# Block attention of a two-layer mixer: its products as split fp32r matmuls, with the query projection ahead of the block compression

## The chip, the cores and the metric

One core of a Trainium2 chip. The metric is device time in microseconds (us) of one execution. In the rows, PE is the matmul engine (TensorE) and PEld its weight loads, DVE the vector engine, ACT the scalar engine, POOL GpSimd, and SP the queue that issues most DMAs.

## What is computed

256 tokens of width 1024 go through feed-forward layers, a first mixer, and then two equal layers, each with a second mixer between feed-forward parts. The second mixer has three attention branches. The change touches the block attention (`nsa_attention`), which itself sums three parts, weighted by per-token gates; `sel` and `win` are causal attention with keys and values of their own:

```python
q = qk_norm(x @ w_q)            # 8 heads of 64, rope on 16 of them
k_c, v_c = compress(k, v)       # blocks of 16 tokens, stride 8: an MLP with weights w1
o_c = softmax(mask_c(q @ k_c.T / 8)) @ v_c
o_s = softmax(causal(q @ k_s.T / 8)) @ v_s     # 2 groups, 4 heads each
o_w = softmax(causal(q @ k_w.T / 8)) @ v_w
o = g[..., 0] * o_c + g[..., 1] * o_s + g[..., 2] * o_w
```

All of it is fp32. In this cut the two causal parts are written as they come out for 256 tokens.

## The kernel before

The tokens are two tiles `t` of 128. A weight comes by DMA on SP as 128x1024 into `raw` (four buffers), is copied to its high part `hi` in fp32r by ACT (L212) and subtracted to its low part `lo` by DVE (L214). A dense product is three fp32r matmuls of 512 columns (L227 hi by high input, L228 lo by high input, L229 hi by low input). So each weight costs ACT and DVE about a microsecond apiece, and PE works behind both. The order of instructions on each engine is set at build time by a scheduler that follows the program's order and the pools; nothing reorders at run time.

The names in the rows end in the section of the program: `ckv` (keys and values, and the loads and splits of the compression weights w1, L942 to L949, into `gl` tiles), `cmp` (the compression, L951 to L994), `nq` (the query projection, L996 to L1009), `dsa` (another branch), `nsa` (the block attention, L1028 to L1089), `gate` (gate projections, whose matmuls are placed between the small ones of `dsa` and `nsa`), `br` and `wo`. In layer 0 the sections named here lie at about 760 to 905 us, and in layer 1 in the same order at about 1390 to 1535 us.

In `nsa` a score is a plain fp32 matmul of 64 rows and 128 columns (L496), and the product of probabilities and values one of 128 rows and 64 columns (L526). An fp32 matmul leaves two records in the trace. A *unit* here is one score bank of 128x512: four heads of tile 0, or two heads of tile 1. Per unit come a mask matmul (L483), maximum (L502), exponential, four transposes (L462), a copy of these (L470), and the products. Each part's output is then scaled and added on DVE (L1057, L1086, L1087), and the sum is transposed again for the output projection (`tp_gate<-ident,ob_nsa`, L265).

`tc.issue_after(after)` holds the first score matmuls behind the last transpose of the queries. PSUM pools: `at` 2 buffers, `tp` 2, `po` 1, `mm` 3.

Of the kernel before, what the change touches and what calls it, by code (L numbers as in the profile page):

```python
# [8 lines left out]
F32 = mybir.dt.float32  # L9
# [108 lines left out]
class K:  # L118
# [78 lines left out]
    def load(self, w, r0, nk, c0, n, pool=None):  # L197

        nc = self.nc
        raw = self.tile(self.wpool, [P, nk, n], "raw", bufs=RAW)  # L200
        parts, m = ([(w, c0)], n) if not isinstance(w, list) else (w, n // len(w))
        for i, (v, c) in enumerate(parts):
            nc.sync.dma_start(out=raw[:, :, m * i:m * i + m],
                              in_=v[r0:r0 + nk * P, c:c + m].rearrange("(k p) n -> p k n", p=P))
# [516 lines left out]
    def mixer2(self, l, nxt):  # L721
# [7 lines left out]
        with ExitStack() as outer:  # L729
# [44 lines left out]
            wi = [I([P, 8], f"wi{t}") for t in range(2)]  # L774
# [16 lines left out]
            gate = [T([P, 24], f"ngate{t}") for t in range(2)]  # L791
# [18 lines left out]
            for t in range(2):  # L810
# [18 lines left out]
                for r in range(8):  # L829
                    m8 = I([P, 8], "m8", 2)  # L830
                    nc.vector.max(out=m8, in_=acc)
                    nc.vector.match_replace(out=acc, in_to_replace=m8, in_values=acc, imm_value=MARK)
# [70 lines left out]
            kT = T([P, 2, S], "kT")  # L903
            vS = [T([P, 2, P], f"vS{t}") for t in range(2)]

            def k_evac(t, ps, br):
                c0 = 256 * (1 - br)
                k = T([P, 2, 64], "selk", 4)
# [3 lines left out]
                self.transposes([k.rearrange("p g d -> p (g d)")], kT[:, br:br + 1, toks[t]])  # L912

            def c_evac(t, ps):
# [4 lines left out]
                self.scaled(vS[t][:, 0], ps[:, 384:512], xs[t][2])  # L919
# [10 lines left out]
            def s_evac(t, ps):  # L930
                k_evac(t, ps, 1)
                self.scaled(vS[t][:, 1], ps[:, 128:256], xs[t][2])

            self.proj(xs, w, 1792, 256, s_evac)


# [16 lines left out]
            vcW = T([P, 8, 64], "vcW")  # L953
            for v in range(2):
                Xv = XS[:, 2 * v:2 * v + 2].rearrange("p g (c b r) -> p g c b r", b=8, r=2)
                hp = self.at((64, 2, P))
                for a in range(2):
# [7 lines left out]
                    ox = I([P, 8, 2, 32], "PT", 3, F32R)  # L965
# [17 lines left out]
                if v == 0:  # L983
                    kc = I([P, 1, 64], "kc")
                    self.head_norm(kc, cp[:, None, :], 1.0, gC[:, None, :])
                    self.rope(kc, c["cosc"], c["sinc"], 8)
                    kd = I([32, 2, 64], "kd", 2)
                    nc.vector.tensor_copy(kd, kc[:32].to_broadcast([32, 2, 64]))
                    p = self.tp((P, 32))
                    nc.tensor.transpose(p, kd.rearrange("p r d -> p (r d)"), self.ident[:32, :32])  # L990
                    nc.vector.tensor_mul(kcT, p, c["bmk"])
                else:
                    nc.vector.tensor_mul(vcW, cp[:, None, :].to_broadcast([P, 8, 64]),
                                         c["bmv"][:, :, None].to_broadcast([P, 8, 64]))  # L994

            self.sec = "nq"  # L996

            nqT = T([P, 4, S], "nqT")

            def nq_evac(t, ps):  # L1000
                tok = T([P, 4, 2, 64], "tok", 3)
                q = tok.rearrange("p j g d -> p (j g) d")
                self.head_norm(tok, ps.rearrange("p (g j d) -> p j g d", g=2, j=4), xs[t][2],
                               gQ[:, None, None, :].to_broadcast([P, 4, 2, 64]))
                self.rope(q, *cs(t, 16), 8)
                self.transposes([tok[:, j].rearrange("p g d -> p (g d)") for j in range(4)], nqT[:, :, toks[t]])

            self.proj(xs, w, 768, 512, nq_evac)
            after = self.lastT  # L1009

# [3 lines left out]
            for t in range(2):  # L1014
# [4 lines left out]
                rd = T([P, 4], "rdc", 2)  # L1019
                for heads, pt, den in self.softmax_banks(mp, t, [[0, 2], [1, 3]], qk, mask, 0.125, ""):  # L1020
                    nc.vector.reciprocal(rd[:, heads[0]:heads[-1] + 1:2], den)
                    PT = self.prob_T(lp, t, pt, "c", 2)
# [7 lines left out]
            ob = []  # L1030
            for t in range(2):
                gt = gate[t].rearrange("p (h b) -> p h b", b=3)
                sc = self.at((P, P))
                with tc.issue_after(after):
                    nc.tensor.matmul(sc, cb["identb"], cb["cmask"][:, toks[t]], start=True, stop=False)
                for j in range(4):
                    nc.tensor.matmul(sc[:, 32 * j:32 * j + 32], nqT[:, j, toks[t]], kcT, start=False, stop=j == 3)
                s3 = sc.rearrange("p (h k) -> p h k", k=16)
# [7 lines left out]
                rd = T([P, 2, 4], "rdb", 2)  # L1046
                nc.vector.reciprocal(rd.rearrange("p g j -> p j g"), den.rearrange("p (j g) -> p j g", g=2))
                rd8 = rd.rearrange("p g j -> p (g j)")
                nc.vector.scalar_tensor_tensor(out=rd8, in0=rd8, scalar=c["cval"][:, t:t + 1], in1=gt[:, :, 0],
                                               op0=OP.mult, op1=OP.mult)  # L1050
                pcT = T([P, 1, P], "pcT", 2)
                self.transposes([pc.rearrange("p h k -> p (h k)")], pcT)
                po = self.po((P, 8, 64))
                nc.tensor.matmul(po.rearrange("p h d -> p (h d)"), pcT[:, 0], vcW.rearrange("p h d -> p (h d)"),
                                 start=True, stop=True)
                o = L([P, 8, 64], f"ob{t}")
                nc.vector.tensor_mul(o, po, rd8[:, :, None].to_broadcast([P, 8, 64]))  # L1057
                ob.append(o)
            pend = []
            for t in range(2):  # L1060
                gt = gate[t].rearrange("p (h b) -> p h b", b=3)
                nh = 4 if t == 0 else 2
                for br in range(2):
                    group = {}
                    rd = T([P, 8], "rdb2", 3)
                    for j0 in range(0, 4, nh):
                        banks = [[4 * g + j for j in range(j0, j0 + nh)] for g in range(2)]
                        qk = lambda h, t=t, br=br: (nqT[64 * (h // 4):64 * (h // 4) + 64, h % 4, toks[t]],
                                                    kT[64 * (h // 4):64 * (h // 4) + 64, br])
                        for heads, pt, den in self.softmax_banks(mp, t, banks, qk, None, 0.125, "", after=after):  # L1070
                            nc.vector.reciprocal(rd[:, heads[0]:heads[-1] + 1], den)
                            PT = self.prob_T(lp, t, pt, "")
                            self.run(pend)

                            def f(heads=heads, PT=PT, t=t, br=br, group=group):
                                if not group:
                                    group["po"] = self.po((P, 8, 64))
                                for i, h in enumerate(heads):
                                    self.pv(group["po"][:, h], PT, i, t,
                                            lambda b: vS[b][:, br, 64 * (h // 4):64 * (h // 4) + 64])  # L1080
                            pend.append(f)

                    def f(t=t, br=br, group=group, rd=rd, gt=gt):
                        nc.vector.tensor_mul(rd, rd, gt[:, :, 1 + br])
                        tmp = T([P, 8, 64], "rl", 2)
                        nc.vector.tensor_mul(tmp, group["po"], rd[:, :, None].to_broadcast([P, 8, 64]))  # L1086
                        nc.vector.tensor_add(ob[t], ob[t], tmp)  # L1087
                    pend.append(f)
            self.run(pend)  # L1089
# [4 lines left out]
            order = [("c", 2, 2, oc), ("a", 0, 2, oa), ("b", 1, 4, ob)]  # L1094
# [14 lines left out]
            for bi, (name, gi, nk, o) in enumerate(order):  # L1109
                oT = []  # L1110
                for t in range(2):
                    hi = self.tile(late, [P, nk, P], f"oTh{bi}{t}", F32R)
                    lo = self.tile(late, [P, nk, P], f"oTl{bi}{t}", F32R)
                    self.split_T(o[t] if nk == 2 else o[t].rearrange("p h d -> p (h d)"), hi, lo)
# [4 lines left out]
            for bi, (name, gi, nk, o) in enumerate(order):  # L1119
# [3 lines left out]
                ws = [self.load(G("w_br_" + name), k * P, 1, 0, D) for k in range(nk)]  # L1123
# [91 lines left out]
```

## Time and profile before

| | us |
|---|---|
| median of three runs | 1787.68 |
| all three | 1787.64, 1787.68, 1796.57 |
| the profiled execution | 1790.69 |
| its span, first to last instruction | 1788.9 |
| mean granted TensorE clock of the profiled execution | 0.993 of full |

The profiled execution stands 3.0 us above the median, and 1.8 us of it lie outside its span. Times in the rows count from the span's start. Because PE's matmuls are pipelined, a matmul's own duration overlaps the next one's; what it costs is the distance from its start to the next start. The same holds on DVE, by less.

### The profile page before, as it was taken

The page shows a single profiled execution, that of the slowest core. Times are in us where ns is not written, and L with a number is a line of the kernel's source. Part 1 is how long each engine was busy: PE and PEld are TensorE (multiplying, and loading weights), DVE is VectorE, ACT ScalarE, POOL GpSimd, SP SyncE. Part 2 cuts the span into 40 slices and gives each one's busy share as a digit, 9 for nine tenths or more (in the row PEclk, how much of TensorE's full clock was granted, in tenths as well). Part 3 has the DMA queues.
Part 4 walks back from the last instruction along what each step waited for, and adds up shares of the span by engine and source line. Part 5 has one row for each costly group of instructions (what it writes and reads, how often), then busy time and mean ns, then how long its engine had stood idle before and what let it go on. Part 6 is the DMA issues. An engine that isn't in the chain of part 4 may idle for free.

```text
span 1788.9 us, 22896 instructions
## 1 busy us (share of the span) xinstructions
PE 1765.3 (99%) x8595; PEld 1453.9 (81%) x8595; DVE 1079.4 (60%) x1706; ACT 897.2 (50%) x1359; POOL 25.8 (1%) x42
## 2 busy tenths in 40 slices
PE   8999999999999999999999999999999999999999
PEld 7888787788878888787888888888887878888887
DVE  5555566555565555797567555655556975575553
ACT  5444455444444444575555444444544755554442
POOL 0000100000000000000000000000000000000000
PEclk9999999999999999999999999999999999999999
DMA  8665654266556655454255665666555442556653
GB/s 281 183 187 192 190 136 142 90 205 188 181 184 195 183 187 192 143 146 125 72 176 178 210 188 182 204 179 188 182 186 155 142 130 69 179 165 203 186 187 130
DMA packets 154991, 305.07 MB, mean 171 GB/s; under 512 B 14040, under 2 KB 45344, under 8 KB 154880
## 3 DMA queue, kind: packets, MB, share of 16 engines
q1 hardware_dynamic: 154864, 303.61, 55.2%
q8 instruction: 67, 1.10, 0.2%
q14 instruction: 44, 0.36, 0.1%
q10 hardware_dynamic: 16, 0.00, 0.0%
HBM read 302.53 MB, written 1.05 MB: 170 GB/s over the span
## 4 chain that ended last, share of the span: by engine, by line
PE 93%; DVE 3%; DMA 2%; ACT 1%; issue 1%; SPq 0%; POOL 0%; POOLq 0%; ACTq 0%
PE mm_ffn L227 10%; PE mm_ffn L229 10%; PE mm_ffn L228 10%; PE at_ffn L229 9%; PE at_ffn L227 9%; PE at_ffn L228 9%; PE mm_gate L228 3%; PE mm_gate L229 2%; PE mm_gate L227 2%; PE at_nsa L496 1%; PE mm_m L228 1%; PE mm_m L227 1%; PE mm_m L229 1%; PE po_nsa L526 1%; PE tp_ffn L265 1%; PE po_ffn L265 1%
## 5 line engine op out<-in xcount | busy, mean ns | idle before, releaser
L214 DVE TENSOR_TENSOR lo_ffn<-raw_ffn,hi_ffn 128x1024 fp32r<-128x1024 f32 x396 | 482.8, 1224 | 455.1 <-ACT hi_ffn L212 453.8
L212 ACT CAST hi_ffn<-raw_ffn 128x1024 fp32r<-128x1024 f32 x396 | 415.2, 1053 | 506.2 <-PE at_ffn L229 307.6
L227 PE MATMUL mm_ffn<-hi_ffn,xh_ffn 128*128 128x512 f32 x288 | 113.1, 393 | 2.5 <-ACT xh_ffn L306 1.3
L228 PE MATMUL mm_ffn<-lo_ffn,xh_ffn 128*128 128x512 f32 x288 | 112.8, 392 | 0.0
L229 PE MATMUL mm_ffn<-hi_ffn,xl_ffn 128*128 128x512 f32 x288 | 112.7, 391 | 0.0
L228 PE MATMUL mm_ffn<-lo_ffn,ah_ffn 128*128 128x512 f32 x264 | 103.8, 393 | 0.0
L227 PE MATMUL mm_ffn<-hi_ffn,ah_ffn 128*128 128x512 f32 x264 | 103.3, 391 | 0.0
L228 PE MATMUL at_ffn<-lo_ffn,ah_ffn 128*128 128x512 f32 x264 | 103.1, 391 | 0.0
L229 PE MATMUL at_ffn<-hi_ffn,al_ffn 128*128 128x512 f32 x264 | 102.9, 390 | 0.0
L227 PE MATMUL at_ffn<-hi_ffn,ah_ffn 128*128 128x512 f32 x264 | 102.8, 389 | 0.0
L229 PE MATMUL mm_ffn<-hi_ffn,al_ffn 128*128 128x512 f32 x264 | 102.8, 389 | 0.0
L227 PE MATMUL at_ffn<-hi_ffn,xh_ffn 128*128 128x512 f32 x240 | 94.5, 394 | 0.0
L229 PE MATMUL at_ffn<-hi_ffn,xl_ffn 128*128 128x512 f32 x240 | 93.5, 390 | 0.0
L228 PE MATMUL at_ffn<-lo_ffn,xh_ffn 128*128 128x512 f32 x240 | 93.4, 389 | 0.0
L214 DVE TENSOR_TENSOR lo_gate<-raw_gate,hi_gate 128x1024 fp32r<-128x1024 f32 x48 | 58.5, 1218 | 35.5 <-ACT hi_gate L212 35.5
L228 PE MATMUL mm_gate<-lo_gate,xh_ffn 128*128 128x512 f32 x192 | 76.9, 401 | 0.7 <-DVE lo_gate L214 0.7
L227 PE MATMUL mm_gate<-hi_gate,xh_ffn 128*128 128x512 f32 x192 | 76.8, 400 | 0.0
L229 PE MATMUL mm_gate<-hi_gate,xl_ffn 128*128 128x512 f32 x192 | 76.3, 399 | 0.0
L228 PE MATMUL mm_ffn<-lo_ffn,xh_wo 128*128 128x512 f32 x192 | 74.9, 390 | 0.0
L229 PE MATMUL mm_ffn<-hi_ffn,xl_wo 128*128 128x512 f32 x192 | 74.7, 389 | 0.0
L227 PE MATMUL mm_ffn<-hi_ffn,xh_wo 128*128 128x512 f32 x192 | 74.7, 389 | 0.0
L212 ACT CAST hi_gate<-raw_gate 128x1024 fp32r<-128x1024 f32 x48 | 50.4, 1051 | 40.1 <-PE mm_gate L229 38.4
(565 smaller groups left out, 3892.3 us busy)
## 6 DMA issues: line engine op xcount, KB each, us to landing
raw_ffn<-in_ffn_w_gu_dram SPq DMA_DIRECT2D x160, 512.0 KB, 3.7
raw_ffn<-in_ffn_w_down_dram SPq DMA_DIRECT2D x132, 512.0 KB, 3.3
raw_gate<-in_w_gate_dram SPq DMA_DIRECT2D x48, 512.0 KB, 3.6
raw_ffn<-in_ffn_w_gate_dram SPq DMA_DIRECT2D x40, 512.0 KB, 4.2
raw_ffn<-in_ffn_w_up_dram SPq DMA_DIRECT2D x40, 512.0 KB, 3.7
raw_m<-in_w_in_dram SPq DMA_DIRECT2D x22, 512.0 KB, 3.8
raw_ffn<-in_ffn_w_gu_dram SPq DMA_DIRECT2D x32, 256.0 KB, 3.2
raw_wo<-in_w_out_dram SPq DMA_DIRECT2D x16, 512.0 KB, 3.3
```

What stands on the lines that cost most here:

```text
L212: nc.scalar.copy(hi, raw)
L214: nc.vector.tensor_sub(lo, raw, hi.bitcast(F32))
L227: nc.tensor.matmul(out, xh, wh, start=first, stop=False)
L228: nc.tensor.matmul(out, xh, wl, start=False, stop=False)
L229: nc.tensor.matmul(out, xl, wh, start=False, stop=last)
L265: nc.tensor.transpose(p[:, i], src[:, i * P:(i + 1) * P], self.ident)
L496: nc.tensor.matmul(sc[:, i, c], q, k[:, c], start=False, stop=i == len(heads) - 1 and b in (t, None))
L526: self.nc.tensor.matmul(out, PT[:, i * (t + 1) + b], v(b), start=b == 0, stop=b == t)
```

## The change

- The section `nq` moves ahead of the loads and splits of w1 and ahead of `cmp`.
- A transposed query is stored stacked, in `qS`: its high part (ACT copy) in the 64 rows of its group, the low part (DVE subtraction) in the other 64. A key is stored as `kh` (high part in both halves) and `kl` (low part in its own half, zeros from POOL in the other). A score for two key blocks is then two fp32r matmuls of 128 rows and 256 columns.
- Values are split (`vh`, `vl`). The probabilities are multiplied by gate over denominator on DVE before they are transposed, the transposed block is split (ACT copy, DVE subtraction), and six fp32r matmuls of 256 columns per unit add all parts into one `po` bank per tile, already transposed. The scaling and adding of outputs on DVE and the eight transposes of `ob` go.
- The compressed scores become eight matmuls of 16 columns per tile instead of four of 32, their product with the values four of 128 columns instead of one of 512.
- The branch's output weight is loaded as two halves of 64 rows (four more DMAs per layer).

```diff
+            kh = T([P, 2, 2, S], "sT", 1, F32R)
+            kl = T([P, 2, 2, S], "kl", 1, F32R)
...
+                p = self.tp([P, P])
+                nc.tensor.transpose(p, k.rearrange("p g d -> p (g d)"), self.ident)
+                for g in range(2):
+                    own, other = half[g], half[1 - g]
+                    nc.scalar.copy(kh[own, g, br, toks[t]], p[own])
+                    nc.scalar.copy(kh[other, g, br, toks[t]], p[own])
+                    nc.vector.tensor_sub(kl[own, g, br, toks[t]], p[own], kh[own, g, br, toks[t]].bitcast(F32))
...
+            def v_evac(t, ps, br):
+                src = ps.rearrange("p (g d) -> p g d", d=64)
+                hi, lo = vh[t][:, br, 0::2], vl[t][:, br, 0::2]
+                self.scaled(hi, src, xs[t][2])
+                nc.vector.scalar_tensor_tensor(out=lo, in0=src, scalar=xs[t][2], in1=hi.bitcast(F32),
+                                               op0=OP.mult, op1=OP.subtract)
...
+            self.sec = "nq"
+
+            qS = T([P, 8, S], "qS", 1, F32R)
+
+            def nq_evac(t, ps):
...
+                for g in range(2):
+                    own, other = half[g], half[1 - g]
+                    dst = qS[:, 4 * g:4 * g + 4, toks[t]]
+                    nc.scalar.copy(dst[own], p[own])
+                    nc.vector.tensor_sub(dst[other], p[own], dst[own].bitcast(F32))
+
+            self.proj(xs, w, 768, 512, nq_evac)
+            after = self.lastT
...
-            self.sec = "nq"
-
-            nqT = T([P, 4, S], "nqT")
...
-            self.proj(xs, w, 768, 512, nq_evac)
-            after = self.lastT
...
+                for i in range(2):
+                    q = qS[:, 4 * g + j0 + i, toks[t]]
...
+                    with tc.issue_after(after) if t == 1 and i == 0 else nullcontext():
+                        nc.tensor.matmul(sc[:, i], q, hi, start=t == 1 and i == 0, stop=False)
+                    nc.tensor.matmul(sc[:, i], q, lo, start=False, stop=t == 0 and i == 1)
...
+                nc.vector.tensor_mul(pw, pw, rd[:, :, None].to_broadcast([P, n, w]))
...
+                nc.scalar.copy(ph, p)
+                nc.vector.tensor_sub(pl, p, ph.bitcast(F32))
...
+                        nc.tensor.matmul(out, wh, ph[:, x], start=False, stop=False)
+                        nc.tensor.matmul(out, wl, ph[:, x], start=False, stop=False)
+                        nc.tensor.matmul(out, wh, pl[:, x], start=False, stop=last and x == 1)
```

How this moves instructions shows at two places, each told for layer 0. The first is DVE between the low part of the last query weight and the low part of the second gate weight. Before, 27 instructions reach from one start to the other; the last of them, where `gl_ckv` are w1 parts, `zs`, `PT` and `kd` work of the compression, and `lo_gate` is a gate weight's low part:

```order
L948 TENSOR_TENSOR gl_ckv_6744<-raw_ckv_6739,gl_ckv_6744 128x4x128
L1157 TENSOR_SCALAR kd_cmp_6785<-tp_cmp_6782 128x32
L967 TENSOR_TENSOR PT_cmp_6825<-zs_cmp_6821,PT_cmp_6825 128x8x32
L1159 TENSOR_SCALAR kd_cmp_6785<-kd_cmp_6785 128x32
L961 TENSOR_TENSOR zs_cmp_6836<-gl_ckv_6456,peT_pn_5817 128x8x15
L1160 RECIPROCAL kd_cmp_6785<-kd_cmp_6785 128x32
L214 TENSOR_TENSOR lo_gate_7512<-raw_gate_7509,hi_gate_7511 128x1024
```

In the changed kernel 62 instructions lie there; a piece of them, on the way to the second gate low part, `lo_gate_7630` (`cop` is what `PT` was, `qS` the queries' low parts, `gl_nq` a w1 part):

```order
L1019 TENSOR_TENSOR cop_cmp_6937<-zs_cmp_6933,cop_cmp_6937 128x8x32
L462 TENSOR_TENSOR tok_nq_6852<-tok_nq_6852,sm_nq_6859 128x512
L1013 TENSOR_TENSOR zs_cmp_6989<-gl_ckv_6454,peT_pn_5817 128x8x15
L431 TENSOR_TENSOR ropeb_nq_6869<-tok_nq_6852,cf_ffn_1602 128x8x8
L432 TENSOR_TENSOR ropeb_nq_6869<-tok_nq_6852,cf_ffn_1602 128x8x8
L983 TENSOR_TENSOR qS_nq_6746<-tp_nq_6843,qS_nq_6746 64x4x128
L433 TENSOR_TENSOR ropea_nq_6868<-tok_nq_6852,cf_ffn_1602 128x128
L1000 TENSOR_TENSOR gl_nq_6904<-raw_nq_6899,gl_nq_6904 128x4x128
L434 TENSOR_TENSOR tok_nq_6852<-ropea_nq_6868,ropeb_nq_6869 128x8x16
```

All eight w1 low parts (three before), all of the queries' normalisation, rope and split (none before) and eight `zs` additions now stand between the two weights.

The second place is PE, at the first use of that gate weight. Before:

```order
L227 MATMUL mm_gate_7489<-hi_gate_7493,xh_ffn_5696 128x512
L228 MATMUL mm_gate_7489<-lo_gate_7494,xh_ffn_5696 128x512
L229 MATMUL mm_gate_7489<-hi_gate_7493,xl_ffn_5697 128x512
L227 MATMUL mm_gate_7489<-hi_gate_7511,xh_ffn_5696 128x512
L228 MATMUL mm_gate_7489<-lo_gate_7512,xh_ffn_5696 128x512
L229 MATMUL mm_gate_7489<-hi_gate_7511,xl_ffn_5697 128x512
```

In the changed kernel:

```order
L233 MATMUL mm_gate_7607<-hi_gate_7629,xh_ffn_5696 128x512
L233 MATMUL mm_gate_7608<-hi_gate_7629,xh_ffn_5771 128x512
L1021 MATMUL at_cmp_6917<-gl_nq_6885,cop_cmp_6922 64x256 x2
L978 MATMUL tp_nq_6843<-ident,tok_nq_6821 128x128 x4
L1021 MATMUL at_cmp_6917<-gl_nq_6885,cop_cmp_6922 64x256 x2
L1021 MATMUL at_cmp_6917<-gl_nq_6888,cop_cmp_6922 64x256 x4
L1021 MATMUL at_cmp_6917<-gl_nq_6893,cop_cmp_6937 64x256 x4
L1021 MATMUL at_cmp_6917<-gl_nq_6896,cop_cmp_6937 64x256 x4
L978 MATMUL tp_nq_6874<-ident,tok_nq_6852 128x128 x4
L1028 MATMUL tp_cmp_6950<-cf_ffn_1602,kd_cmp_6948 128x32 x2
L234 MATMUL mm_gate_7607<-lo_gate_7630,xh_ffn_5696 128x512
```

From the first use of the last query weight's low part to this matmul PE had 37 matmuls and now has 52: seven more gate matmuls of 512 columns and the eight query transposes; the 16 `at_cmp` are in both.

## Rows read from the trace of the kernel before

**Rows 1.** The page's first part: busy time, share of the span and instructions of each engine.

```profile
PE 1765.3 (99%) x8595; PEld 1453.9 (81%) x8595; DVE 1079.4 (60%) x1706; ACT 897.2 (50%) x1359; POOL 25.8 (1%) x42
```

**Rows 2.** Groups by line on PE: out<-in, shape, count | busy us, mean ns.

```profile
L496 PE MATMUL at_nsa<-kT_ckv,nqT_nq 64*128 64x128 f32 x192 | 28.5, 292 | 0.0
L526 PE MATMUL po_nsa<-vS_ckv,PT_nsa 128*128 128x64 f32 x192 | 27.0, 271 | 0.0
...
L1037 PE MATMUL at_nsa<-kcT_cmp,nqT_nq 128*128 128x32 f32 x32 | 4.1, 272 | 0.0
...
L265 PE MATMUL tp_gate<-ident,ob_nsa 128*128 128x128 f32 x16 | 2.2, 279 | 0.0
```

**Rows 3.** PE's timeline in `nsa`: start us, us, instruction.

```profile
840.00 0.38 PE L483 MATMUL at_nsa<-cb 128*128 128x512 bf16 x1
840.31 1.16 PE L496 MATMUL at_nsa<-kT_ckv,nqT_nq 64*128 64x128 f32 x8
841.39 1.13 PE L1054 MATMUL po_nsa<-vcW_cmp,pcT_nsa 128*128 128x512 f32 x2
...
864.83 1.00 PE L526 MATMUL po_nsa<-vS_ckv,PT_nsa 128*128 128x64 f32 x8
865.67 0.27 PE L483 MATMUL at_nsa<-cb 128*128 128x256 bf16 x1
```

**Rows 4.** PE's timeline in `ckv`, first and last of a run of 41.

```profile
782.50 0.28 PE L227 MATMUL mm_ckv<-hi_ckv,xh_ffn 128*128 128x256 f32 x1
...
787.28 0.28 PE L228 MATMUL mm_ckv<-lo_ckv,xh_ffn 128*128 128x256 f32 x1
```

**Rows 5.** Windows: us, busy us of PE, PEld, DVE, ACT, POOL, PEclk, DMA share, GB/s.

```profile
760.00:770.00 10.00, 10.00 (x65) 8.98 (x64) 9.86 (x29) 5.97 (x12) 0.00 (x0) 1.00 0.53 155
...
800.00:810.00 10.00, 9.66 (x57) 7.73 (x56) 9.84 (x29) 7.71 (x16) 0.62 (x2) 1.00 0.69 218
...
850.00:860.00 10.00, 10.00 (x73) 7.93 (x72) 6.59 (x17) 5.95 (x26) 0.00 (x0) 1.00 0.17 53
```

**Rows 6.** DVE's timeline in `ckv`, `cmp` and `nq`: start us, us, instruction.

```profile
793.86 0.16 DVE L425 TENSOR_TENSOR ropeb_ckv<-selk_ckv,cf_ffn 128x16 f32<-128x16 f32 x1
...
794.37 0.34 DVE L453 SCALAR_TENSOR_TENSOR selk_ckv<-mm_ckv,rs_ffn,gS_pn 128x128 f32<-128x128 f32 x1
...
797.49 1.23 DVE L214 TENSOR_TENSOR lo_nq<-raw_nq,hi_nq 128x1024 fp32r<-128x1024 f32 x1
...
801.36 1.22 DVE L214 TENSOR_TENSOR lo_gate<-raw_gate,hi_gate 128x1024 fp32r<-128x1024 f32 x1
802.50 0.42 DVE L967 TENSOR_TENSOR PT_cmp<-zs_cmp,PT_cmp 128x256 fp32r<-128x256 f32 x1
802.83 1.29 DVE L948 TENSOR_TENSOR gl_ckv<-raw_ckv,gl_ckv 128x512 fp32r<-128x512 f32 x2
804.03 0.90 DVE L961 TENSOR_TENSOR zs_cmp<-gl_ckv,peT_pn 128x120 f32<-128x120 f32 x3
804.87 0.67 DVE L948 TENSOR_TENSOR gl_ckv<-raw_ckv,gl_ckv 128x512 fp32r<-128x512 f32 x1
...
806.82 1.16 DVE L214 TENSOR_TENSOR lo_gate<-raw_gate,hi_gate 128x1024 fp32r<-128x1024 f32 x1
...
811.14 0.48 DVE L453 SCALAR_TENSOR_TENSOR tok_nq<-mm_nq,rs_ffn,gQ_pn 128x256 f32<-128x256 f32 x1
811.53 0.15 DVE L442 TENSOR_TENSOR sm_cmp<-sm_cmp,sm_cmp 128x1 f32<-128x1 f32 x1
```

**Rows 7.** PE's timeline, the first use of the second gate low part, in both layers.

```profile
808.03 0.50 PE L228 MATMUL mm_gate<-lo_gate,xh_ffn 128*128 128x512 f32 x1 [0.34 <-DVE lo_gate L214]
...
1435.95 0.50 PE L228 MATMUL mm_gate<-lo_gate,xh_ffn 128*128 128x512 f32 x1 [0.32 <-DVE lo_gate L214]
```

**Rows 8.** Windows and PE's timeline in the first mixer, after a wait.

```profile
214.15 0.50 PE L228 MATMUL mm_m<-lo_m,xh_ffn 128*128 128x512 f32 x1 [2.69 <-DVE lo_m L214]
...
215.40:218.80 3.40, 3.40 (x9) 2.65 (x8) 2.82 (x6) 2.25 (x4) 0.00 (x0) 0.50 0.88 242
```

More of the change, by code (lines that the diff above doesn't have):

```diff
@@ L201, in load @@
         parts, m = ([(w, c0)], n) if not isinstance(w, list) else (w, n // len(w))
-        for i, (v, c) in enumerate(parts):
-            nc.sync.dma_start(out=raw[:, :, m * i:m * i + m],
-                              in_=v[r0:r0 + nk * P, c:c + m].rearrange("(k p) n -> p k n", p=P))
+        if isinstance(r0, list):
+            p0 = 0
+            for r, k in r0:
+                nc.sync.dma_start(out=raw[p0:p0 + k, 0], in_=w[r:r + k, c0:c0 + n])
+                p0 += k
+        else:
+            for i, (v, c) in enumerate(parts):
+                nc.sync.dma_start(out=raw[:, :, m * i:m * i + m],
+                                  in_=v[r0:r0 + nk * P, c:c + m].rearrange("(k p) n -> p k n", p=P))
         if pool is None:
@@ L773, in mixer2 @@
             iT = I([P, 3, S], "iT")
-            wi = [I([P, 8], f"wi{t}") for t in range(2)]
+            wi = I([P, 2, 8], "wi")
+            wi = [wi[:, t] for t in range(2)]
             def idx_evac(t, ps):
@@ L790, in mixer2 @@
             dv = [T([P, 64], f"dv{t}") for t in range(2)]
-            gate = [T([P, 24], f"ngate{t}") for t in range(2)]
+            gate = T([P, 2, 24], "ngate")
+            gate = [gate[:, t] for t in range(2)]
             def dsa_evac(t, ps):
@@ L990, in mixer2 @@
                     nc.tensor.transpose(p, kd.rearrange("p r d -> p (r d)"), self.ident[:32, :32])
[L991 removed]
+                    nc.vector.tensor_copy(kcT, p)
                 else:
[L993 to L1009 removed]
+                    for g in range(2):
+                        nc.vector.tensor_mul(vcW[:, :, g], cp[:, None, :].to_broadcast([P, 4, 64]),
+                                             c["bmv"][:, 4 * g:4 * g + 4, None].to_broadcast([P, 4, 64]))
             self.sec = "dsa"
@@ L1018, in mixer2 @@
                 mask = M[t][:, None, :].to_broadcast([P, 2, P * (t + 1)])
-                rd = T([P, 4], "rdc", 2)
+                rd = self.sm(4, "rdc")
                 for heads, pt, den in self.softmax_banks(mp, t, [[0, 2], [1, 3]], qk, mask, 0.125, ""):
                     nc.vector.reciprocal(rd[:, heads[0]:heads[-1] + 1:2], den)
-                    PT = self.prob_T(lp, t, pt, "c", 2)
+                    PT = self.tile(lp, [P, 2 * (t + 1), P], "rl", bufs=2)
+                    self.transposes([pt[:, i, b * P:(b + 1) * P] for i in range(2) for b in range(t + 1)], PT)
                     for i, h in enumerate(heads):
@@ L1028, in mixer2, with compressed @@
             self.sec = "nsa"
[L1030 to L1033, printed above, removed]
+            obT = [[L([P, 4, P], f"ob{n}{t}", 1, F32R) for n in "hl"] for t in range(2)]
+            pend = []
+            def compressed(t, po, gt):
+                sc = self.at((P, 4, 2, 16))
                 with tc.issue_after(after):
-                    nc.tensor.matmul(sc, cb["identb"], cb["cmask"][:, toks[t]], start=True, stop=False)
+                    nc.tensor.matmul(sc.rearrange("p j g k -> p (j g k)"), cb["identb"], cb["cmask"][:, toks[t]],
+                                     start=True, stop=False)
                 for j in range(4):
-                    nc.tensor.matmul(sc[:, 32 * j:32 * j + 32], nqT[:, j, toks[t]], kcT, start=False, stop=j == 3)
-                s3 = sc.rearrange("p (h k) -> p h k", k=16)
+                    for g in range(2):
+                        nc.tensor.matmul(sc[:, j, g], qS[:, 4 * g + j, toks[t]].bitcast(F32),
+                                         kcT[:, 16 * g:16 * g + 16], start=False, stop=j == 3 and g == 1)
+                s3 = sc.rearrange("p j g k -> p (j g) k")
                 mx = self.sm(8, "mx")
@@ L1045, in mixer2 @@
                 nc.vector.tensor_reduce(out=den, in_=pc, axis=AX.X, op=OP.add)
[L1046 to L1049, printed above, removed]
+                rd = self.recip(den, 8, "rdb")
+                r3 = rd.rearrange("p (j g) -> p j g", g=2)
@@ L1054, in mixer2 @@
[L1054 to L1059, printed above, removed]
+                for j in range(4):
+                    nc.tensor.matmul(po[:, j], vcW[:, j].rearrange("p g d -> p (g d)"), pcT[:, 0],
+                                     start=j == 0, stop=False)
@@ L1060, in mixer2 @@
             for t in range(2):
                 gt = gate[t].rearrange("p (h b) -> p h b", b=3)
[L1062 to L1088, printed above, removed]
@@ L1089, in mixer2 @@
-            self.run(pend)
+                po = self.po((P, 4, P))
+                compressed(t, po, gt)
+                todo = [(g, j0, br) for g in range(2) for j0 in (0, 2) for br in ([None] if t == 0 else [0, 1])]
+                for k, (g, j0, br) in enumerate(todo):
+                    unit(t, g, j0, br, po, gt, k == len(todo) - 1)
+                self.run(pend)
+                nc.scalar.copy(obT[t][0], po)
+                nc.vector.tensor_sub(obT[t][1], po, obT[t][0].bitcast(F32))
@@ L1122, in mixer2 @@
                 acc = self.accs()
-                ws = [self.load(G("w_br_" + name), k * P, 1, 0, D) for k in range(nk)]
+                if o is None:
+                    ws = [self.load(G("w_br_b"), [(64 * k, 64), (256 + 64 * k, 64)], 1, 0, D) for k in range(nk)]
+                else:
+                    ws = [self.load(G("w_br_" + name), k * P, 1, 0, D) for k in range(nk)]
                 for t in range(2):
```

87 lines of the change are left out of this document (75 added, 12 removed).

## The prediction

> **What bounds the kernel now.** I read the page's busy times first: PE is busy for 1765.3 of 1788.9 us, DVE for 1079.4 and POOL for 25.8 [rows 1]. So a microsecond taken from PE is one gained, as long as its operands are there. Next the groups by line and PE's timeline, to price the products that go and those that come [rows 2 to 4]; the reader is to see starts, not durations, since matmuls overlap. Then windows around the place to which the query projection moves: there DVE is at 9.86 and 9.84 of 10 us, so DVE is the second bound, and PE is barely ahead of it [rows 5]. The starts on DVE price what is put between two weights [rows 6]. What the path is worth there shows in PE's first use of the second gate low part: it already waits 0.34 us in layer 0 and 0.32 in layer 1, for DVE [rows 7]. Since the two layers show the same, each term is worked out for one layer and doubled.
>
> **PE's work, per layer.** Scores: 192 records of two layers, so 96 per layer [rows 2], eight of which take 841.39 - 840.31 = 1.08 us, 0.135 each [rows 3]: 13.0 us go. Probabilities by values: 96 records at (865.67 - 864.83) / 8 = 0.105: 10.1 us go. In their place stand 12 units with four score matmuls and six value matmuls, 120 fp32r matmuls of 256 columns. The nearest rows are the 41 of that size in `ckv`, 40 starts in 787.28 - 782.50 = 4.78 us, 0.1195 each [rows 4]: 14.3 us come. So 8.8 us are saved. The compressed scores go from 16 records [rows 2] to 32, since each query head has a matmul of its own: 16 at 0.105 are 1.7 us back. Their value product keeps its columns and is put at nothing, covered by no one: were it to rise by the 0.03 between the two paces over 16 records, 0.5 us. Eight transposes of `ob` go [rows 2], at 0.105: 0.8. The 12 masks stay; one of 512 columns took 0.31 ahead of a 64-row score [rows 3], against 0.24 by the fp32r pace, so 0.07 each, 0.8. Sum: 8.8 - 1.7 + 0.8 + 0.8 = 8.7 us, **17.4 us less for both layers**.
>
> **The move of the query projection, per layer.** Between the starts of the last query low part (797.49) and the second gate low part (806.82) DVE needs 9.3 us for 27 instructions [rows 6]. Now 62 stand there. Their price from starts [rows 6]: the two weight low parts 1.14 each (802.50 - 801.36), 2.3; sixteen of 512 columns, namely eight w1 parts, two reductions, two multiplications and four query low parts, at 0.60 (two from 802.83 to 804.03), 9.6; four query scalings at 0.39 (811.53 - 811.14), 1.6; eight `zs` at 0.28 (three from 804.03 to 804.87), 2.2; four `cop` at 0.33 (802.83 - 802.50), 1.3. Of the 28 smaller ones, six of 2 to 32 columns take 0.51 (793.86 to 794.37), which would make 2.4; some have 64 or 128 columns, a duration of 0.15 each is nearer to 4.2, and I take 3.6 between these ends. Sum 20.6, which is 11.3 more. PE, for its part, has more to do meanwhile: seven matmuls of 512 columns at 0.23 to 0.24 (two of 256, rows 4) and eight transposes at 0.105, 2.4 us. So PE, which already came 0.34 early, waits 0.34 + 11.3 - 2.4 = 9.2 us; **18.4 for both**. Whether this shows at one gate weight or is spread over two and the high parts on ACT is left open. The work was not new: DVE and ACT did it behind the second gate low part, where PE had split weights in hand. What is late next is the key of the compression, whose chain now stands behind three gate low parts, one more than before: up to 1.1 us at `tp_cmp`, taken at 1.0, 2.0 for both.
>
> **Keys and values.** Four times per layer a key costs two DVE subtractions of 64x128 in place of a copy that ACT and DVE shared, and a value one more instruction of 128x128: ten more per layer, at no more than the 0.34 us that one of 128x128 lasts [rows 6], 3.4 us. They fall where DVE is at 9.86 of 10 [rows 5]. At the lower end they cost nothing, since PE still had 10.00 of 10 there. I take 1.0, 2.0 for both layers, with 0 to 6.8 kept for the range.
>
> **The clock.** In the first mixer a wait of 2.69 us for DVE at 214.15 is followed by a stretch, 215.40 to 218.80, in which the granted clock is 0.50, the 1.2 GHz level, while PE is busy throughout: half of its 3.40 us is lost, 1.7 [rows 8]. The short wait of 0.34 us left the clock at 1.00 in its window [rows 5, 7]. Waits of 9 us in one or two pieces per layer are nearer to the first. Two places per layer make 0 to 6.8 us; I take half, 3.4. The Trainium skill, page "TensorE: Matmul & The Clock Gate", sections "What's actually happening" and "HAM oscillation", says that the half clock is the default, that activity lifts it, and that a wait for data brings it back each time; by it all four would count and the sum be 3.4 us longer. The first mixer agrees with it, the short wait shows its limit.
>
> **What costs nothing.** The scaling of the probabilities and the split of their transposes put 26 DVE instructions of 512 columns per layer where 18 stood, 8 x 0.60 = 4.8 us. The stage is longer than the 25 us between the scores and values of rows 3; over these alone it is 1.9 in 10, on top of the 6.59 of 10 that DVE has there [rows 5]: 8.5 at most, hidden behind gate matmuls. Without this cover all 9.6 would show. The Trainium skill, page "TensorEngine Tiling (Array Packing)", section "PSUM Bottleneck", warns that a faster TensorE can leave PSUM's evacuation as the bound; by it the 17.4 us would not come out, and that is the last rival below. The stage's window speaks against it. POOL's zeros hide in an engine that is 1% busy; the four more DMAs per layer and the query weights, which pass the w1 loads on SP's queue, hide while the DMA share is 0.53 and 0.69 [rows 5]; uncovered, w1 would come late and not a gate weight.
>
> **The sum.** -17.4 + 18.4 + 2.0 + 2.0 + 3.4 = +8.4 us. The profiled execution's 1790.7 becomes 1799.1. It stands 3.0 above the median, so against the median 1787.7 the forecast is **1796.1**. With the unknown terms at their lower ends (no clock, no keys and values, no late chain) it is +1.0, 1788.7; at their upper ends (6.8, 6.8, 2.2) +16.8, 1804.5. About 0.5%, 8.9 us, can be told from no change: 1778.8 and 1796.6 are the bounds, and the forecast lies just inside.
>
> **Rivals.**
> *Slower, through the clock.* PE stops at four places long enough that each is followed by a stretch at 1.2 GHz with PE last. For it speaks the fall after 2.69 us [rows 8]; against it, that a wait split into pieces may leave the clock alone as the 0.34 did. All four falls give 1796.1 + 3.4 = 1799.5, with keys and values at their upper end 1804.3; I put it at 1802, between. It decides once waits and clock together exceed 26.3 us (17.4 + 8.9).
> *Faster: the waits don't form.* The moved work is the same work earlier. If DVE enters the stretch further ahead of PE than before, because PE is held up by its own 15 more matmuls and DVE's queue has no wait for a slow transpose, the 18.4 go and the clock stays: 1787.7 - 17.4 + 4.0 = 1774. Half of the waits give 1783. Against it: DVE at 9.84 of 10 has nothing to run ahead with, and the 0.34 is there already.
> *The products' gain does not appear.* Either a stacked fp32r matmul costs as much as the two records it replaces, or the attention stage waits for its evacuation. Then +8.4 + 17.4: 1813. Rows 4 speak against the first, the window of the stage against the second.
>
> **How the numbers follow.** The forecast's case has 0.60, of which its own range, 1789 to 1804, puts 0.44 within the bounds and 0.16 above. The clock case has 0.20, all slower. Waits that don't form have 0.14: 0.10 faster, 0.04 within. The last has 0.06. So faster 0.10, within 0.48, slower 0.42. The range from 1782 to 1806 leaves out most of the third case below and the fourth above, and a tail of the clock case, together under 0.2.
>
> **What would show it.** In the profile after: scores and value products in groups of 256 columns at 0.12 us from start to start; no multiply-and-add of outputs; PE waits of several us for a gate weight at about 803 to 826 us and again some 628 us later, released by DVE's low part or ACT's high part; DVE at 9.8 or more there; windows with PEclk under 1 right behind. Wrong would be: no PE wait over 1 us there (then 1774), or waits inside `nsa` for probabilities (then the evacuation binds).

## The result, and the profile after

The changed kernel takes **1808.9 us** (median of four runs, 1807.8 to 1810.0) against 1787.7 for the one before; the ratio of the runs is 1.0108, 95% interval 1.0093 to 1.0123. That is slower by 19.3 us on that ratio, above the range of 1782 to 1806. The profiled execution is one at the median, 1808.6.

The first part of its page, which answers to [rows 1]:

```profile
span 1806.7 us, 22854 instructions
...
PE 1758.3 (97%) x8491; PEld 1448.5 (80%) x8491; DVE 1104.0 (61%) x1770; ACT 913.5 (51%) x1405; POOL 29.1 (2%) x54
```

PE is busy for 7.0 us less, in a span that is 17.8 longer: its idle time went from 1788.9 - 1765.3 = 23.6 to 1806.7 - 1758.3 = 48.4, up by 24.8. The groups by line on PE show what replaced [rows 2] (busy us, mean ns):

```profile
L1117 PE MATMUL at_nsa<-sT_ckv,qS_nq 128*128 128x256 f32 x48 | 15.3, 337 | 0.0
L1157 PE MATMUL po_nsa<-cop_nsa,vh_ckv 128*128 128x256 f32 x48 | 15.0, 313 | 0.1
...
L1118 PE MATMUL at_nsa<-kl_ckv,qS_nq 128*128 128x256 f32 x48 | 12.8, 283 | 0.0
...
L1079 PE MATMUL at_nsa<-kcT_cmp,qS_nq 128*128 128x16 f32 x64 | 7.6, 261 | 0.0
```

There are no waits before them to speak of. The list of PE's waits (us in total, times, longest) shows where they went instead:

```profile
PE mm_gate L234 <- DVE lo_gate L220: 11.4, 3, 5.5
PE mm_gate L233 <- ACT hi_gate L218: 7.4, 2, 4.0
...
PE mm_nq L233 <- DVE selk_ckv L434: 2.5, 2, 1.2
...
PE tp_nq L978 <- DVE tok_nq L434: 1.8, 2, 0.9
```

In [rows 7] the second gate low part made PE wait 0.34 and 0.32 us. The same places on PE's timeline after, with a piece of `nsa` that answers to [rows 3]:

```profile
787.29 0.47 PE L233 MATMUL mm_nq<-hi_nq,xh_ffn 128*128 128x512 f32 x1 [1.25 <-DVE selk_ckv L434]
...
806.43 1.22 PE L233 MATMUL mm_gate<-hi_gate,xh_ffn 128*128 128x512 f32 x2 [3.96 <-ACT hi_gate L218]
...
823.14 0.79 PE L234 MATMUL mm_gate<-lo_gate,xh_ffn 128*128 128x512 f32 x1 [5.47 <-DVE lo_gate L220]
...
856.05 0.28 PE L1157 MATMUL po_nsa<-cop_nsa,vh_ckv 128*128 128x256 f32 x1
856.17 0.28 PE L1158 MATMUL po_nsa<-cop_nsa,vl_ckv 128*128 128x256 f32 x1
856.29 0.28 PE L1159 MATMUL po_nsa<-sp_nsa,vh_ckv 128*128 128x256 f32 x1
856.41 0.28 PE L1117 MATMUL at_nsa<-sT_ckv,qS_nq 128*128 128x256 f32 x1
856.52 0.28 PE L1118 MATMUL at_nsa<-kl_ckv,qS_nq 128*128 128x256 f32 x1
...
1443.59 0.76 PE L233 MATMUL mm_gate<-hi_gate,xh_ffn 128*128 128x512 f32 x2 [3.45 <-ACT hi_gate L218]
...
1460.82 0.80 PE L234 MATMUL mm_gate<-lo_gate,xh_ffn 128*128 128x512 f32 x1 [5.47 <-DVE lo_gate L220]
```

Matmuls of 256 columns start 0.12 us apart, as priced. DVE between the two gate low parts of layer 0, on its timeline:

```profile
806.41 1.23 DVE L220 TENSOR_TENSOR lo_gate<-raw_gate,hi_gate 128x1024 fp32r<-128x1024 f32 x1 [1.50 <-ACT hi_gate L218]
...
814.34 0.69 DVE L983 TENSOR_TENSOR qS_nq<-tp_nq,qS_nq 64x512 fp32r<-64x512 f32 x1 [1.60 <-ACT qS_nq L982]
...
821.87 1.22 DVE L220 TENSOR_TENSOR lo_gate<-raw_gate,hi_gate 128x1024 fp32r<-128x1024 f32 x1
```

That is 15.5 us from start to start, 5.5 in [rows 6], and part of it DVE itself waits, for ACT's copy of the transposed queries: the line is long, and it is also held. Windows of the same stretch and of `nsa` (columns as in [rows 5]):

```profile
803.40:806.80 3.40, 0.37 (x1) 0.37 (x2) 1.90 (x6) 1.44 (x3) 0.00 (x0) 0.86 0.48 181
806.80:810.20 3.40, 3.36 (x8) 2.16 (x8) 3.40 (x13) 2.64 (x7) 0.00 (x0) 0.50 0.37 89
810.20:813.60 3.40, 3.40 (x14) 2.73 (x14) 2.53 (x12) 1.05 (x1) 0.62 (x2) 0.63 0.18 70
...
820.40:823.80 3.40, 0.66 (x2) 0.56 (x3) 3.34 (x9) 2.01 (x3) 0.00 (x0) 0.50 0.28 109
823.80:827.20 3.40, 3.40 (x21) 3.36 (x20) 3.37 (x8) 0.76 (x4) 0.00 (x0) 0.62 0.82 228
850.00:860.00 10.00, 10.00 (x69) 8.42 (x67) 8.02 (x20) 7.35 (x29) 0.00 (x0) 1.00 0.39 107
```

The granted clock falls to 0.50, the 1.2 GHz level, twice in each layer here. In the four windows at 0.50 to 0.63 PE's busy time times the missing share is 1.7 + 1.3 + 0.3 + 1.3 = 4.6 us lost, and the same windows of layer 1 give 4.6 again; the last row shows `nsa` at full clock, with DVE at 8.02 of 10 and PE never short of work.

Matching starts of the same matmuls gives the same size for both layers: from 717.89 to 924.67 before and 714.47 to 930.44 after it is +9.2, from there to 1552.61 before and 1568.16 after +9.8, 19.0 in all. So by place, from the first to the last of these points: PE's idle time grows by 23.7 and its busy time falls by 4.8 (826.8 before, 822.0 after). Since the clock added about 2 x 4.6 = 9 to the busy time, PE's work is some 14 us less. The execution of before shown had lost 3.4 us ahead of the first of these points, where the program is the same, most of it in PE's busy time (706.0 against 703.1); that is why the spans differ by less than the medians.

### The profile page after: what moved, and what is told of

It is laid out like the page before. It is cut to its first block, busy times and chain, and to the rows that moved or that the text cites. A ratio compares the mean times of both kernels' runs of the same rounds, so it can differ in the third digit from the quotient of the medians.

```text
span 1806.7 us, 22854 instructions
## 1 busy us (share of the span) xinstructions
PE 1758.3 (97%) x8491; PEld 1448.5 (80%) x8491; DVE 1104.0 (61%) x1770; ACT 913.5 (51%) x1405; POOL 29.1 (2%) x54
## 4 chain that ended last, share of the span: by engine, by line
PE 88%; DVE 6%; DMA 3%; ACT 1%; issue 1%; SPq 0%; POOL 0%; POOLq 0%; ACTq 0%
PE mm_ffn L233 10%; PE mm_ffn L234 10%; PE mm_ffn L235 10%; PE at_ffn L235 9%; PE at_ffn L233 9%; PE at_ffn L234 9%; PE mm_gate L234 3%; PE mm_gate L233 3%; PE mm_gate L235 3%; PE mm_m L234 1%; PE mm_m L233 1%; PE mm_m L235 1%; PE tp_ffn L271 1%; PE po_ffn L271 1%; PE at_m L502 1%
## 5 line engine op out<-in xcount | busy, mean ns | idle before, releaser
L234 PE MATMUL mm_gate<-lo_gate,xh_ffn 128*128 128x512 f32 x192 | 79.6, 414 | 11.5 <-DVE lo_gate L220 11.4
```

Of the source, the lines that this page charges most:

```text
L234: nc.tensor.matmul(out, xh, wl, start=False, stop=False)
```

## The experiments

Each ratio is to the kernel before, of runs on the same chip, with its 95% interval; 0.001 is 1.8 us. Every edit is scheduled anew, so the order of instructions on the engines differs in places from kernel to kernel; where this bears on a reading it is said.

**The two halves of the change.** The first kernel is the changed one with the section `nq` put back behind `cmp`, its text unchanged; the second is the kernel before with only that move.

```diff
-            self.sec = "nq"
-
-            qS = T([P, 8, S], "qS", 1, F32R)
...
-            self.proj(xs, w, 768, 512, nq_evac)
-            after = self.lastT
...
             self.sec = "cmp"
...
+            self.sec = "nq"
+
+            qS = T([P, 8, S], "qS", 1, F32R)
...
+            self.proj(xs, w, 768, 512, nq_evac)
+            after = self.lastT
```

and, in the kernel before:

```diff
+            self.sec = "nq"
+
+            nqT = T([P, 4, S], "nqT")
...
+            self.proj(xs, w, 768, 512, nq_evac)
+            after = self.lastT
...
             self.sec = "cmp"
...
-            self.sec = "nq"
-
-            nqT = T([P, 4, S], "nqT")
...
-            self.proj(xs, w, 768, 512, nq_evac)
-            after = self.lastT
```

> The changed kernel with the query projection put back behind the compression; all else of the change stays. If the move is what costs (through DVE's queue or through the weight buffers), PE's waits for gate weights at 803 to 826 us and 628 us later go, and what is left is the cheaper products: 1771 to 1778 us. If the products or their evacuation cost the time, it stays at 1800 or more with waits inside the block attention.

> The kernel before with only the query projection moved ahead of the w1 loads. If the move is what costs, it alone makes the kernel slower than the changed one, by the products' gain that is missing here: 1812 to 1828 us, with PE waiting several us for gate weights. If the move costs nothing by itself, 1786 to 1790.

e1: 1788.0 us, ratio 0.9987 [0.9974, 1.0001]. e2: 1806.3 us, 1.0094 [1.0069, 1.0118]. The move alone costs 16.8 us, somewhat less than was expected of it; putting it back takes 21.6 off the changed kernel. The waits of PE that e2 has and the kernel before has not:

```profile
PE tp_nq L462 <- DVE tok_nq L428: 5.9, 3, 2.6
PE mm_gate L227 <- ACT hi_gate L212: 4.4, 2, 2.5
```

That is 10.3 us, where the changed kernel waits for 11.4 + 7.4 + 1.8 = 20.6 at the same places. And e1 missed: without the move the products should have made it some 10 to 17 us faster than before, and it is hardly faster at all. Its PE has a wait that the kernel before does not have (the changed kernel has it too, the 1.25 us at 787.29). PE's timeline of e1:

```profile
790.69 0.28 PE L893 MATMUL at_sb<-cop_sb,neg 128*128 128x256 f32 x1
792.58 0.47 PE L233 MATMUL mm_nq<-hi_nq,xh_ffn 128*128 128x512 f32 x1 [1.60 <-DVE selk_ckv L434]
```

What DVE did meanwhile (its timeline):

```profile
790.89 1.02 DVE L895 TENSOR_TENSOR zs_sb<-zs_sb,at_sb 128x256 f32<-128x256 f32 x2 [0.51 <-PE at_sb L891]
...
792.09 0.34 DVE L941 SCALAR_TENSOR_TENSOR vl_ckv<-mm_ckv,rs_ffn,vh_ckv 128x128 fp32r<-128x128 f32 x1
```

And the windows behind it:

```profile
790.00:792.60 2.60, 0.99 (x9) 0.77 (x7) 2.09 (x13) 1.52 (x3) 0.00 (x0) 1.00 0.66 202
790.00:800.00 10.00, 8.39 (x45) 7.15 (x44) 7.02 (x32) 6.15 (x17) 0.56 (x2) 0.83 0.34 105
...
794.50:797.90 3.40, 3.40 (x11) 2.76 (x10) 2.43 (x11) 2.77 (x10) 0.29 (x2) 0.50 0.51 154
```

The wait ends 0.15 us behind L941; the profile names L434, the next in DVE's line, which neither reads `mm` nor feeds the query. The query's first matmul needs a bank of the `mm` pool, which has three; its last reader is the value's low part, read from `mm_ckv` on DVE, and that stands in line behind the additions of another branch and the rope. In the kernel before, a value left that bank by one instruction of ACT. Then the clock falls and 1.7 us more go, in each layer. PE goes on to wait for gate low parts too, 1.3 us in all. That the extra DVE instructions are the cause was then tried directly.

**Without the low parts of keys and values.** e1 without their subtractions, the tiles zeroed once instead:

```diff
-                    nc.vector.tensor_sub(kl[own, g, br, toks[t]], p[own], kh[own, g, br, toks[t]].bitcast(F32))
...
-                nc.vector.scalar_tensor_tensor(out=lo, in0=src, scalar=xs[t][2], in1=hi.bitcast(F32),
-                                               op0=OP.mult, op1=OP.subtract)
```

> The kernel of e1 (query projection back) without the subtractions that make the low parts of keys and values: those parts are zero, written once by POOL, so the scores and outputs lack them; PE does the same matmuls. If the keys' and values' low parts on DVE are what takes the products' gain back, it falls by their waits and the slower clock behind them, 5 to 7 us per layer: 1774 to 1779 us. If the gain is lost elsewhere (the attention stage, the gates), 1786 to 1790.

1776.1 us, 0.9918 [0.9897, 0.9939]: as expected. The wait is gone, and the window that stood at 8.39 of 10 and clock 0.83 in e1 is full:

```profile
790.00:800.00 10.00, 10.00 (x57) 8.17 (x55) 9.35 (x41) 8.13 (x24) 0.56 (x2) 1.00 0.42 116
```

So the products and all the rest are worth 0.0082 x 1787.7 = 14.7 us, and 24 DVE instructions that last 7.3 us together (16 keys of 0.286, 8 values of 0.342 in the changed kernel) take back (0.9987 - 0.9918) x 1787.7 = 12.3, with some 4.5 to either side.

**The value out of PSUM at once.** One ACT instruction takes the scaled value to a buffer in SBUF; high and low part are made from there. e5 does it in e1, e9 in the changed kernel.

```diff
-                self.scaled(hi, src, xs[t][2])
-                nc.vector.scalar_tensor_tensor(out=lo, in0=src, scalar=xs[t][2], in1=hi.bitcast(F32),
-                                               op0=OP.mult, op1=OP.subtract)
+                f = T([P, 2, 64], "pcT", 2)
+                self.scaled(f, src, xs[t][2])
+                nc.scalar.copy(hi, f)
+                nc.vector.tensor_sub(lo, f, hi.bitcast(F32))
```

> The kernel of e1 (query projection back), but the value leaves its PSUM bank by one ACT instruction into a staging tile, and high and low part are made from there. Bank theory (the value's low part on DVE, in line behind other work, holds the bank that the query projection's first matmul needs): PE's 1.60 us wait at that matmul and the stretch at a granted clock of 0.83 behind it go, 3 us per layer: 1780 to 1784 us. Load theory (ten more DVE instructions in a stretch where DVE is full, wherever they stand): the wait moves to the next weight, 1786 to 1789.

> The changed kernel, query projection first, with only the values staged as in e5. If the values' hold on the PSUM bank costs here what it does in e1, 1803 to 1806 us. If PE's time is set by the queue between the gate weights, which this does not touch, the bank's 1.25 us wait goes and comes back later: 1806 to 1810.

e5: 1783.8 us, 0.9958 [0.9941, 0.9974], **faster than both kernels**, and 5 us less than e1, with some 4 to either side. e9: 1797.4 us, 1.0046 [1.0031, 1.0061], 11 us less than the changed kernel. The wait `mm_nq` for `selk_ckv` is in neither. In e5 DVE has as many instructions as in e1 (the eight low parts last 0.28 us each in place of 0.35) and the low part still stands behind the same additions and most of the rope, but no longer holds the bank; ACT has eight instructions more. That shows the held bank, apart from the load. In e5 PE still waits 3.2 us for `lo_nq` and 1.7 for `cop_cmp`, so the load is likely a part too.

e9 gained more than either theory gave, and it does not show the bank alone, because its order is another one: the first two gate low parts of layer 0 start 2.7 us apart on DVE (814.88 and 817.62), where it was 15.5 in the changed kernel, and none of PE's longest waits is for a gate low part. How much of its 11 us is the bank and how much the order was not told apart. Its list has

```profile
PE tp_nq L979 <- DVE tok_nq L434: 5.8, 2, 3.0
PE mm_gate L233 <- ACT hi_gate L218: 4.9, 2, 2.4
PE at_cmp L1022 <- DVE cop_cmp L1020: 4.4, 2, 2.3
```

**Was it the weights' buffers, not DVE?** In the changed kernel ACT waits 2.90 us for the DMA of a gate weight (`raw_gate`) just before the 3.96 of PE. The w1 loads use the same ring of four; e3 gives them buffers of their own. e4 leaves the buffers and puts `nq` between the w1 loads and `cmp`.

```diff
-                    raw = self.tile(self.wpool, [P, 8, P], "raw", bufs=RAW)
...
-                        r = raw[:, 4 * i:4 * i + 4]
+                        r = T([P, 4, P], "P", 3)
+                        m0 = 1024 * a + 512 * i
+                        nc.sync.dma_start(out=r, in_=G("nsa_cmp_w1")[v, m0:m0 + 512]
+                                          .rearrange("(m p) h -> p m h", p=P))
```

and for e4:

```diff
+            w1 = []
+            for v in range(2):
...
             self.sec = "nq"
...
-            w1 = []
-            for v in range(2):
...
             self.sec = "cmp"
```

> The changed kernel with the w1 parts loaded in halves into the P buffers, so that the four raw buffers serve only dense weights; the order of the work stays. Queue theory (DVE has 11 us more to do between two gate weights): the waits stay, 1804 to 1810 us. Ring theory (w1 loads hold raw buffers until DVE has split them, so gate weights are loaded late and their transfer time is in the open): ACT no longer waits some 3 us for raw_gate, PE's waits for gate weights halve, 1794 to 1800.

> The changed kernel with the query projection between the w1 loads and the compression. Ring theory: the raw buffers go through w1, queries, gates in the order of before, so gate weights are not held by w1; 1790 to 1798 us. Queue theory: eight w1 low parts (4.8 us per layer, three of them were there before) leave the stretch, the queries' 8 us stay in it: 1798 to 1804.

e3: 1807.8 us, 1.0098 [1.0074, 1.0122], no change. ACT's wait for that DMA fell to 0.17 us, and PE's moved:

```profile
PE tp_nq L978 <- DVE tok_nq L434: 10.2, 4, 2.7
PE mm_gate L233 <- ACT hi_gate L218: 2.8, 2, 1.4
```

The ring is not the cause: PE's idle time is less by 5.8 us (42.6 in place of 48.4), but its busy time is longer by 7.2 at a lower granted clock (0.985 in place of 0.988). What PE waits for is mostly DVE's line, under whatever name comes next in it. e4: 1800.1 us, 1.0059 [1.0038, 1.008]: two fifths of the 21.6 us are gone, and PE waits for `cop_cmp` (7.0 us in all) and `tok_nq` (5.1), the same line in another order.

**The line relieved by POOL.** The low parts of w1 go to POOL: in the changed kernel (e7), and in e5 together with those of the values (e6).

```diff
-                        nc.vector.tensor_sub(u[:, :, 1], r, u[:, :, 0].bitcast(F32))
+                        nc.gpsimd.tensor_sub(u[:, :, 1], r, u[:, :, 0].bitcast(F32))
```

> The changed kernel, with the low parts of w1 on POOL in place of DVE and nothing else: 4.8 of the 20.6 us leave DVE's queue between the two gate weights. Queue theory: PE's waits there shrink by 3 to 5 us per layer, 1799 to 1804 us. If the waits come from transfers or ACT, it stays at 1806 to 1811.

> e5 with the low parts of values and of w1 made on POOL in place of DVE, 5.8 us of DVE work per layer. Load theory: the waits for DVE at 790 to 820 us go, and the products' 17 to 19 us come out: 1770 to 1776 us. Bank theory: little beyond e5, 1779 to 1784. If POOL is too slow for w1, the compression waits for it and it is above e5.

e7: 1795.7 us, 1.003 [1.0019, 1.0041], 14 us less than the changed kernel, where 6 to 10 were expected. DVE's busy time did not fall, 1103.9 us against 1104.0, since other instructions last longer (below). What fell is the line between the first two gate low parts of layer 0, from 15.5 us to 2.9 (807.42 and 810.37), and PE no longer waits for `lo_gate`. So it is DVE's line, by what stands in it and where, and not by the sum of its work. e6 is a miss: 1808.0 us, 1.0096 [1.0077, 1.0115], 25 us more than e5. PE waits there for gate low parts (5.6 us) and for ACT's evacuation of a gate (4.6). The timelines of e6 show what DVE and POOL do. DVE:

```profile
770.97 1.27 DVE L877 TENSOR_TENSOR sp_sb<-sp_sb,cf_ffn 128x256 f32<-128x256 f32 x1
...
773.82 0.41 DVE L839 MAX8 sm_top<-iacc_top 128x8 f32<-128x256 f32 x1
774.16 1.18 DVE L877 TENSOR_TENSOR sp_sb<-sp_sb,cf_ffn 128x256 f32<-128x256 f32 x1
...
778.61 1.91 DVE L220 TENSOR_TENSOR lo_ckv<-raw_ckv,hi_ckv 128x1024 fp32r<-128x1024 f32 x1
```

and POOL:

```profile
770.66 1.30 POOL L978 TENSOR_TENSOR gl_ckv<-raw_ckv,gl_ckv 128x512 fp32r<-128x512 f32 x1 [49.71 <-ACT gl_ckv L977]
773.49 1.56 POOL L978 TENSOR_TENSOR gl_ckv<-raw_ckv,gl_ckv 128x512 fp32r<-128x512 f32 x1 [1.53 <-ACT gl_ckv L977]
776.38 3.06 POOL L978 TENSOR_TENSOR gl_ckv<-raw_ckv,gl_ckv 128x512 fp32r<-128x512 f32 x2 [1.32 <-ACT gl_ckv L977]
```

The product (L877) that lasts 1.27 and 1.18 us here takes 0.42 in the kernel before, the low part of 1.91 takes 1.22. They stretch where POOL runs, and end 0.3 us after POOL's instruction does (772.24 behind 771.96, 775.34 behind 775.05). This begins at 770 us, and just ahead of that DVE stood at 9.86 of 10 in the kernel before [rows 5]; in e7 POOL begins at 788. The stretching is there too (a rope addition of 128x32 at 1.20 us in place of 0.18), and e7 gains in spite of it. In e6 DVE is busy for 1103.6 us with 24 instructions less than in e5, where it is 1099.3. How much of the 25 us comes from the stretching was not told apart.

**The same with the keys.** e10 is e5 with the key staged by ACT and its low parts on POOL; e11 has those of the values there too.

```diff
+                f = T([P, P], "pcT", 2)
+                nc.scalar.copy(f, p)
...
-                    nc.vector.tensor_sub(kl[own, g, br, toks[t]], p[own], kh[own, g, br, toks[t]].bitcast(F32))
+                    nc.gpsimd.tensor_sub(kl[own, g, br, toks[t]], f[own], kh[own, g, br, toks[t]].bitcast(F32))
```

> e5 (query projection back, values staged) with the keys staged too and their low parts made on POOL: eight DVE subtractions of 64x128 per layer leave DVE. Load theory: e5 gave back about half of what e8 did by leaving the low parts out; this brings the other part, 1777 to 1781 us, under e5 and under the kernel before. If POOL's subtractions hold up DVE or ACT's extra copy holds up the keys, 1783 to 1790.

> e10 with the values' low parts on POOL as well, four more DVE instructions of 128x128 per layer: 1775 to 1780 us if DVE's load decides, above e10 if POOL gets in DVE's way.

Both missed: 1795.2 us, 1.0033 [1.002, 1.0045], and 1792.0 us, 1.0017 [1.0007, 1.0028], slower than e5. PE's waits in e10:

```profile
PE po_sb L901 <- ACT zs_sb L896: 3.3, 2, 1.7
PE at_sb L888 <- ACT rl_sb L881: 2.7, 4, 1.2
PE mm_ckv L233 <- ACT pcT_ckv L422: 1.8, 2, 0.9
```

Now ACT is late, for another branch's rows and for the staging buffer `pcT`. Whether ACT's added copies, the two staging buffers or POOL's hold on DVE are to blame was not told apart.

## Why the prediction was wrong

The sum's sign, +8.4, was right and its size was not: keys and values were priced far too low, and the clock too, while the waits of the move were priced too high.

- **PE's work: right in kind, somewhat too large.** Forecast 8.7 per layer. Starts are 0.12 apart, as rows 4 gave; by place some 14 us of the 17.4 came, and by e8 14.7, with whatever else the new evacuation costs in it.
- **Nothing in `nsa` for the evacuation: right.** DVE rose to 8.02 of 10 in the window that was forecast at up to 8.5, and PE did not wait. The last rival, 1813, falls, though its time is the nearest to the median that came.
- **The move's waits: right in place and kind, in size by luck.** PE was forecast to wait 9.2 us per layer at the gate weights, released by the low part or the high part, and 1.0 behind them at `tp_cmp`. It waits 3.96 and 5.47, with 0.9 behind, at `tp_nq` and not at `tp_cmp` (0.18). DVE's line of 62 instructions, priced at 20.6 us, took 25.4 (796.51 to 821.87), in which DVE is busy for 21.9 and waits for ACT. But alone (e2) the move makes PE wait for 10.3 us in both layers and costs 16.8, less than the 18.4 + 2.0 + 3.4 set down for it with the clock. The other half of the waits in the changed kernel comes only when the rest of the change is there, so the match with 18.4 is two errors that cancel.
- **Keys and values: the step that failed.** "I take 1.0 per layer", 2.0 in all with 6.8 at most, is 12.3 in e8. The bound was the length of the instructions, 0.34 each, on an engine at 9.86 of 10, and the argument for the lower end was that PE stood at 10.00 of 10 there. The length is not the price. A low part read from PSUM keeps a bank of `mm` until an instruction far back in DVE's line has read it, and the next projection cannot start; in e1 PE then stops for 1.60 us for an instruction of 0.34, and the clock drops. PE at 10.00 of 10 was no cover, since PE had no slack to hide a late bank in. The held bank is 5 of the 12.3, by e5; the other 7 are the rest of what these instructions do to DVE's line, which was not taken apart further. No run takes the low parts out of the changed kernel itself, where the waits at their own places (`mm_nq`, `tp_ckv`) are only 3.7 us and the rest would stand in the waits at the gates.
- **The clock: mis-sized.** 3.4 was half of four falls at 1.7; the falls came at all four places, and each took part of a second window (0.63, 0.62) too, about 9 us in all. By place this term is the one that is furthest off. The clock case was thus right about the falls, and low in its price. The Trainium skill, page "TensorE: Matmul & The Clock Gate", section "HAM oscillation", has a kernel's waits for data bring the half clock back each time: the four long waits here agree. Behind the short wait of 1.25 us at 787.29 PEclk stays at 1.00, so not every wait does it.

By cause, the parts give -14.7 + 12.3 + 16.8 = +14.4 against the measured 19.3. The gap of 4.9, or 0.0108 + 0.0013 - 0.0094 = 0.0027 of the time, is no more than the three intervals together leave uncertain (0.0032); whether the two halves add up exactly or make each other worse stays open. A wait of 1.4 us for `hi_wo` late in layer 1, new in the profile after, is in it and was not followed up.

## What to carry to other kernels

Price an instruction that reads PSUM by the bank it keeps, and by the line in which it stands, not by its length: look for the next matmul group that needs the bank, and where the two engines stand neck and neck let one instruction empty the bank first (e5 against e1, at the same count of DVE instructions). A section moved ahead of another takes its whole evacuation with it into the line of the engine that splits weights; test the two halves of such a change apart, since here the gain of the one lay under two losses of about its own size. Compare the order of instructions too before a gain is put down to one cause, since an edit of a few lines can move a whole stretch (e7, e9). An idle engine is no free help where it stretches the instructions of the busy one: low parts on POOL took 14 us off one kernel (e7) and added 25 to another (e6).

## What was not expected of the hardware

- Work on POOL lengthens some DVE instructions by 0.7 to 1.1 us and leaves others alone: the product of two SBUF operands went from 0.42 to 1.27 us, and the low part of 1024 columns from 1.22 to 1.91, while MAX8, with one operand, kept its 0.41 us in the middle of a POOL instruction (773.82). The Trainium skill, page "SBUF — State Buffer", section "SBUF: two separate sides", says that a DVE instruction with two SBUF inputs and a GpSimd instruction that reads SBUF exclude each other for the whole of an instruction; the stretched rows shown agree, each having two inputs in SBUF. Two inputs are not the only case: in e7 a TENSOR_SCALAR with one input (`sm_nq`, 128x8) took 1.25 us at 812.53, 0.16 where POOL is idle, while POOL worked from 810.24 to 813.76. POOL's own 128x512 subtractions take 1.30 to 2.06 us in e6.
- The clock did not follow the length of a single wait. It stayed at 1.00 behind 1.25 us in the profile after, and fell behind 1.60 us in e1 and behind waits of 0.85 and 0.96 us within 3 us of each other in e5:

```profile
798.00:801.40 3.40, 1.65 (x10) 0.97 (x9) 3.31 (x12) 3.07 (x8) 0.31 (x1) 1.00 0.03 13
801.40:804.80 3.40, 3.27 (x8) 2.59 (x9) 3.11 (x8) 1.46 (x5) 0.31 (x1) 0.50 0.63 161
```

In the window ahead of the fall PE was busy for 1.65 of 3.40 us. In layer 1 of the same execution PE waits 0.84 and 0.97 us at the same two places, 1424.54 and 1427.03, and the clock stays at 1.00 there; so the length of the waits alone does not tell what the clock will do.
